# Reordering the first transfers of a two-layer hybrid decoder step on eight cores

## The chip, the cores and the metric

The kernel runs as one program on all 8 cores of one Trainium2 chip. Every core works on its own sequence, and no core talks to another. The metric is the device time of the slowest core, in microseconds (us). Repeated executions of one kernel mostly agree within a few tenths of a per cent (20 runs of the kernel before: 665.77 to 670.74 us, all within 0.5% of their median). Now and then an execution falls into a slow state, in which cores of one die show a lower clock. A median that is quoted is that of all runs.

## The reference

The reference is one inference step of a two-layer trunk (`D_MODEL = 1024`, 2048 prompt rows and 64 sample rows on each core). In each layer an input projection feeds three groups of heads, and an output projection follows:

```python
h = rms_norm(x, norm_g)
p = einsum('ntd,de->nte', h, w_in)          # IN_WIDTH = 3456 columns
a_val, a_gate, a_z, b_h, b_b, b_c, b_z, c_u, c_v, c_z = split(p)
# group A: GLU, causal depthwise conv of width 31, LayerNorm, silu, gate
a = a_val * sigmoid(a_gate)
y_a = silu(layer_norm(causal_dwconv(a_buf, a, a_conv_w) + a_conv_b)) * silu(a_z)
# group B: gated causal conv of width 3
y_b = b_b * causal_dwconv(b_buf, b_c * b_h, b_conv_w) * silu(b_z)
# group C: 128x128 causal mixing of LayerNorm(c_v) inside chunks of 128 rows
y_c = c_u * chunk_mix(layer_norm(c_v), c_ws, c_bs) * silu(c_z)
x = x + einsum('nte,ed->ntd', concat(y_a, y_b, y_c), w_out)
```

It returns the final RMS norm of both streams and the last rows of the convolution states.

## The kernel before

The rows of a core are cut into blocks of up to 512 columns. A block has three or four tiles of x, each with 128 rows; the last tile of block 1 has the 64 sample rows. The kernel records every operation with what it reads and writes. A scheduler then sets the order in each engine's queue, and adds semaphores. `after=` adds a dependence on an operation, which here serves to hold back a transfer. `mark()` is the last operation recorded for TensorE.

Each engine that starts transfers has a queue of its own to the 16 DMA engines: SyncE's (`"sp"`, q1 in the profile), ScalarE's (`"act"`, q10) and GpSimd's (`"pool"`, q0, which casts the weights to bf16 on the way).

```python
        def dma(q, out, in_, reads, writes, after=()):
            # ... S.add(q, lambda e: e.dma_start(out=out, in_=in_), ..., dma=True, after=after)

        def load_x(l, t, after=(), q="sp"):                 # one tile of x, 512 KB
            # ...
            dma(q, xr[0:r, s, :], src[r0:r0 + r, :], [] if l == 0 else [("x1", t)], [("x", s)], after)

        def load_win(l, i, after=()):                       # a piece of w_in, on GpSimd's queue
            # ...
        def load_wout(l, hf, after=()):                     # half of w_out, on GpSimd's queue
            dma("pool", w_out_sb[:, hf, :, :]..., wo_ap(w_out.tensor, l * 2 * 128 * 4096, hf, GO[l]), [],
                [("wout", hf)], after)

        def params_dma(l, after=()):                        # nine small transfers on SyncE's queue
            dma("sp", wc4[:, :], wcol[l], [], ["wc4"], after)
            dma("sp", wraw[:], c_wsT[l], [], ["wraw"], after)
            # ... wr4, gC_b, bC_b, and cbias in four parts
```

The sums of squares of a block's x are ScalarE's work. The powers `rstd` follow on GpSimd, and `h_tm = x * rstd` on VectorE:

```python
        def H_elem(l, blk):
            for j, (t, r, c0) in enumerate(blk.tiles):
                # ...
                act(h_tm[0:r, hs, :], xr[0:r, s, :], AF.Square, [("x", s)], [("htm", hs), ("ss", k)],
                    scale=1.0 / 32.0, accum=ss[0:r, k:k + 1])
                rsq(rstd[0:r, k:k + 1], ss[0:r, k:k + 1], 1, ...)   # two GpSimd instructions, save in block 0
                ts(h_tm[0:r, hs, :], xr[0:r, s, :], rstd[0:r, k:k + 1], ...)
```

The start:

```python
        for t in blocks[0].ids:
            load_x(0, t, (), "act" if t % 2 else "sp")
            if t == 1:
                dma("sp", cst[:], consts, [], ["cst"])
                dma("act", pc[:], pcols, [], ["pc"])
            if t == 2:
                xmark = [S.ops[-1].idx]
        params_dma(0)
        # ... memsets
        for i in range(len(PIECES)):                        # 13 pieces of w_in
            load_win(0, i, xmark if i >= 1 else ())
        dma("sp", a_scr.rearrange("c p t -> p c t")[:, :, 0:PADA], zpad[:], ["zpad"], [("azero",)])
        H_elem(0, blocks[0])
        # ... transposes, and the first projections of block 0 in two halves of 256 columns
```

The loop over blocks. Group A's product is stored to the scratch tensor `a_scr` and loaded back as `A4` in a layout that the depthwise convolution needs. The profile calls this load `A<-a_scr`:

```python
        for oi, (l, blk) in enumerate(order_b):
            # ...
            stage_A(l, blk, ...)                            # projections, GLU, store to a_scr
            mA = mark()
            a4 = [a4_load(l, blk, c, False) for c in range(3)]       # 12 loads on SyncE's queue
            # ... stage_Bz, stage_AZ, stage_O(*prev)
            mO = mark()
            if nxt is not None:
                for t in nxt[1].ids:
                    load_x(nxt[0], t, mA)
                    if l == 0 and blk.first and t == nxt[1].ids[2]:
                        xmark = [S.ops[-1].idx]
                if l == 0 and blk.first:
                    for hf in range(2):
                        load_wout(0, hf, xmark)             # held back until a tile of block 1's x has landed
            stage_CV(l, blk)                                # group C: variances, rstdc on GpSimd, nv
            mC = mark()
            if blk.first:
                hist_dma(l, mC)                             # loads zst, and casts it on GpSimd
            # ...
            if nxt is not None:
                H_elem(*nxt)                                # squares of the next block's x
            for c in range(3):
                stage_B(l, blk, c)
            stage_C(l, blk)
            if nxt is not None:
                pcb = [balloc() for _ in range(3)]
                convs(l, blk, a4, pcb, [0])                 # first convolution
                T(*nxt, 0); T(*nxt, 1)                      # transposes of the next block (cut: one a line)
                convs(l, blk, a4, pcb, [1])
                T(*nxt, 2); T(*nxt, 3)
                convs(l, blk, a4, pcb, [2])                 # third convolution
```

## Time and profile before

| before | value |
|---|---|
| time, median of 6 runs ahead of the prediction | 667.9 us |
| span of the profiled run, slowest core (core 6) | 665.7 us |
| spans of the eight cores | 659.7 to 665.7 us |
| TensorE busy over the span | 91% |
| TensorE busy in the first 110 us | about 70 us |

Of TensorE's 61 us of idle time, 40 us lie in the first 110 us. After that it waits for other engines for only 10.9 us, and much of the rest is the end of the kernel, where it has little left to do (11.9 us of work after 640 us). So the start is where a transfer order can matter. The table by stretches of the kernel before, core 6, shows it. Its columns are the stretch in us, its length, the busy time of each engine with its instructions, the granted share of TensorE's clock, the busy share of the DMA engines (values a little over 1 are read as full) and their rate.

```profile
core 6: us, PE busy (x) PEld busy (x) DVE busy (x) ACT busy (x) POOL busy (x), PEclk, DMA share, GB/s
0.00:20.00 20.00, 1.89 (x16) 1.62 (x16) 4.39 (x19) 7.24 (x16) 4.16 (x11) 1.00 0.71 173
20.00:40.00 20.00, 17.54 (x113) 11.42 (x114) 6.63 (x10) 5.85 (x11) 5.88 (x10) 1.00 1.04 169
40.00:60.00 20.00, 19.17 (x105) 9.78 (x102) 3.83 (x7) 1.32 (x2) 0.00 (x0) 1.00 1.03 172
60.00:80.00 20.00, 7.17 (x24) 2.75 (x24) 6.03 (x10) 8.01 (x15) 5.64 (x11) 0.66 0.84 176
80.00:100.00 20.00, 13.84 (x92) 6.12 (x92) 10.99 (x23) 2.98 (x6) 2.52 (x4) 0.83 0.73 140
```

TensorE has a hole at 60 to 80 us with only 7.17 us of work, and the clock falls there to 0.66. The list of TensorE's waits over the first 110 us of the same core names what ended each hole (what was waited for; total us; how many times; the longest):

```profile
PE pb L444 <- ACT tmp L404: 13.7, 1, 13.7
PE pb L892 <- DVE h_tm L417: 13.0, 1, 13.0
PE pb L444 <- ACT h_fm L404: 7.6, 2, 5.8
PE pb L444 <- DVE nv L420: 6.2, 1, 6.2
```

The 13.0 us are the wait for the first x, which can't be avoided entirely, since all work starts from it. The 13.7 us end with an instruction of ScalarE. The timeline of the same core (start, length, engine, line, operation, and in brackets the idle time before it and what ended it) says why ScalarE was late:

```profile
44.84 2.67 SPq L434 DMA_DIRECT2D xr<-x_in  x4
...
70.54 1.06 ACT L404 ACTIVATE h_tm<-xr 128x1024 bf16<-128x1024 f32 x1 [26.78 <-DMA xr<-x_in]
...
72.83 7.25 PE L444 MATMUL pb<-h_fm,w_in_sb 128*128 128x512 bf16 x24 [13.66 <-ACT tmp L404]
...
92.32 1.91 PE L445 MATMUL pb<-A,W 128*32 128x512 bf16 x32
94.17 7.08 PE L444 MATMUL pb<-h_fm,w_in_sb 128*128 128x512 bf16 x32
...
101.08 1.68 PE L565 MATMUL pb<-ident_bf,h_tm 128*128 128x128 bf16 x16
...
106.16 1.91 PE L445 MATMUL pb<-A,W 128*32 128x512 bf16 x32
```

ScalarE reaches the first square of block 1 at 43.8 us and stands there for 26.78 us, until that tile of x has landed. Behind it in its queue stand evacuations of PSUM that TensorE needs: instructions that copy TensorE's results out of their buffer (`pb`), so that the buffer is free again. The convolutions of block 0 are the groups of 32 matmuls `pb<-A,W`: the first starts at 92.32 us and the third at 106.16 us.

The x tile is late because it is issued only at 44.84 us, and because the DMA engines are full from 20 to 70 us (DMA share 1.02 to 1.04 in each 10 us). I counted the packets of the trace's packet records, in the microsecond from 48 to 49 us:

```
queue of GpSimd (weights):  44 packets, 36 of them of 4096 bytes
queue of SyncE:             45 packets, of 1080 bytes
```

So the DMA engines give the two queues one packet each in turn here, 4096 bytes against 1080. Three queues at work had the like: from 11 to 12 us of the same core, those of SyncE, ScalarE and GpSimd had 23, 24 and 23 packets. This does not hold everywhere in these records: at 20 to 21 us of the same core, when the weights had only begun, 389 packets of SyncE's queue (mostly of 64 and 512 bytes) passed beside 29 of the weights.

### The profile page before, as it was taken

What the parts mean: (1) busy time and instruction counts of PE and PEld (TensorE: products, weight loads), DVE (VectorE), ACT (ScalarE), POOL (GpSimd) and SP (SyncE); (2) the same over time, 40 slices, a digit from 0 to 9 for tenths busy, and PEclk for the clock granted to TensorE, in tenths of its full rate; (3) what the DMA queues carried; (4) which work ended last, traced back from release to release, by engine and by line L of the source; (5) the groups of instructions that cost most, each with busy time, mean ns of one, the idle gap of its engine ahead of it and who ended that gap; (6) DMA issues with size and microseconds to landing.
All of it is one profiled execution on the core that took longest, in us unless ns stands there. A gap on an engine that the chain in (4) does not pass through costs nothing.

```text
span 665.7 us, 11443 instructions; the slowest of 8 cores (659.7 to 665.7 us)
## 1 busy us (share of the span) xinstructions
PE 604.6 (91%) x4484; PEld 331.2 (50%) x4484; DVE 380.8 (57%) x710; ACT 268.3 (40%) x472; POOL 90.6 (14%) x163
## 2 busy tenths in 40 slices
PE   1695489999989999999998999999989999999974
PEld 0543135555545565655553544545555565665631
DVE  2240544956267475573756663977278666764774
ACT  2410516601443462272263315731474274272632
POOL 0500400201012011000223310022002002100101
PEclk9998679999999999999999999999999999999988
DMA  7899760962597359149869590532462033324202
GB/s 192 146 180 187 151 140 7 209 196 41 135 193 152 87 107 239 58 116 241 229 83 243 147 172 13 171 108 78 114 184 95 17 112 110 103 45 54 97 0 95
DMA packets 57270, 83.98 MB, mean 126 GB/s; under 512 B 8128, under 2 KB 46208, under 8 KB 56960
## 3 DMA queue, kind: packets, MB, share of 16 engines
q1 hardware_dynamic: 41168, 58.48, 31.4%
q0 software_dynamic: 11392, 19.24, 19.4%
q10 hardware_dynamic: 4656, 5.54, 3.4%
q8 instruction: 35, 0.57, 0.3%
q14 instruction: 19, 0.16, 0.1%
HBM read 80.59 MB, written 27.62 MB: 163 GB/s over the span
## 4 chain that ended last, share of the span: by engine, by line
PE 78%; DMA 10%; DVE 4%; ACT 4%; issue 2%; SPq 1%; POOL 1%; POOLq 0%; ACTq 0%; DVEq 0%
PE pb L444 68%; PE pb L445 7%; DMA xr<-x_in 6%; DMA xr<-x_scr 3%; PE pb L565 3%; ACT tmp L404 1%; ACT L404 1%; SPq L434 1%; DVE tmp L424 1%; DMA a_scr<-a_t 1%; ACT h_tm L404 1%; DVE nv L420 1%; ACT h_fm L404 0%; DVE xr L412 0%; DVE vb L773 0%
## 5 line engine op out<-in xcount | busy, mean ns | idle before, releaser
L444 PE MATMUL pb<-h_fm,w_in_sb 128*128 128x384 bf16 (+3 forms) x2032 | 372.6, 343 | 27.1 <-ACT tmp L404 17.2
L444 PEld LDWEIGHTS pb<-h_fm,w_in_sb 128*128 128x128 bf16 x2032 | 196.8, 99 | 189.8 <-ACT tmp L404 18.5
L404 ACT ACTIVATE tmp<-pb 128x384 f32<-128x384 f32 (+2 forms) x110 | 56.7, 519 | 201.5 <-PE pb L444 191.1
L444 PE MATMUL pb<-w_out_sb,mix 128*128 128x512 bf16 (+1 forms) x544 | 120.6, 382 | 4.0 <-DVE mix L412 4.0
L444 PEld LDWEIGHTS pb<-w_out_sb,mix 128*128 128x128 bf16 (+1 forms) x544 | 53.7, 99 | 68.6 <-DVE mix L412 4.4
L424 DVE SCALAR_TENSOR_TENSOR tmp<-z_ext,pc,tmp 128x384 f32<-128x384 bf16 (+1 forms) x60 | 38.1, 641 | 55.2 <-ACT tmp L404 54.6
L412 DVE TENSOR_TENSOR xr<-pb,xr 128x512 f32<-128x512 f32 (+1 forms) x68 | 46.3, 688 | 34.0 <-PE pb L444 33.6
L404 ACT ACTIVATE h_tm<-xr 128x1024 bf16<-128x1024 f32 (+1 forms) x34 | 35.7, 1051 | 64.8 <-DMA xr<-x_in 46.7
L543 POOL TENSOR_SCALAR rstd<-ss 128x1 f32<-128x1 f32 (+1 forms) x47 | 12.1, 257 | 363.3 <-ACT h_tm L404 251.8
L445 PE MATMUL pb<-A,W 128*32 128x384 bf16 (+2 forms) x1152 | 49.3, 314 | 0.0
L412 DVE TENSOR_TENSOR mix<-tmp 128x384 bf16<-128x384 f32 (+2 forms) x50 | 30.1, 602 | 27.6 <-ACT tmp L404 27.5
L424 DVE SCALAR_TENSOR_TENSOR a_t<-tmp,pb 128x384 bf16<-128x384 f32 (+1 forms) x30 | 16.8, 561 | 47.8 <-ACT tmp L404 43.2
L404 ACT ACTIVATE tmp<-xr 128x1024 bf16<-128x1024 f32 (+1 forms) x17 | 18.0, 1057 | 51.4 <-DVE xr L412 51.4
L412 DVE TENSOR_TENSOR tmp<-pb,tmp 128x384 f32<-128x384 f32 (+2 forms) x50 | 29.4, 591 | 13.4 <-PE pb L444 13.0
L417 DVE TENSOR_SCALAR h_fm<-pb,pc 128x384 bf16<-128x384 bf16 (+3 forms) x44 | 17.8, 416 | 33.2 <-PE pb L565 24.0
L445 PEld LDWEIGHTS pb<-A,W 128*32 128x32 bf16 x1152 | 24.9, 96 | 19.0 <-issue 4.5
L444 PE MATMUL pb<-w_in_sb,h_fm 128*128 128x256 bf16 (+1 forms) x272 | 31.8, 273 | 0.9 <-ACT szt L404 0.9
L404 ACT ACT_TABLE_LOAD x22 | 28.2, 1283 | 8.5 <-DMA xr<-x_in 8.2
L773 DVE RECIPROCAL vb<-vb 128x384 f32<-128x384 f32 (+2 forms) x10 | 27.9, 2792 | 4.2 <-ACT vb L404 3.9
L544 POOL TENSOR_TENSOR rstd<-rstd,mhalf 128x1 f32<-128x1 f32 (+1 forms) x47 | 29.3, 624 | 3.9
L404 ACT ACTIVATE h_fm<-pb,pc 128x384 bf16<-128x384 bf16 (+3 forms) x44 | 24.9, 580 | 12.3 <-PE pb L892 7.1
L444 PEld LDWEIGHTS pb<-w_in_sb,h_fm 128*128 128x128 bf16 (+1 forms) x272 | 26.4, 99 | 6.9 <-ACT szt L404 1.1
(73 smaller groups left out, 449.2 us busy)
## 6 DMA issues: line engine op xcount, KB each, us to landing
A<-a_scr SPq DMA_DIRECT2D x96, 103.0 KB, 4.3
w_in_sb<-w_in POOLq DMA_DIRECT2D x17, 512.0 KB, 16.4
x_scr<-xr SPq DMA_DIRECT2D x16, 512.0 KB, 4.6
xr<-x_scr SPq DMA_DIRECT2D x16, 512.0 KB, 6.3
y_o<-xr SPq DMA_DIRECT2D x16, 512.0 KB, 2.7
xr<-x_in SPq DMA_DIRECT2D x14, 512.0 KB, 14.1
w_out_sb<-w_out POOLq DMA_DIRECT2D x4, 1024.0 KB, 15.2
w_in_scr<-w_in POOLq DMA_DIRECT2D x7, 512.0 KB, 13.7
```

Source lines behind the costliest of these rows:

```text
L404: S.add("act", lambda e: e.activation(out=out, in_=in_, func=func, **kw), reads=reads, writes=writes, cost=170 + 0.833 * free_size(out) + ...
L412: S.add(eng, lambda e: e.tensor_tensor(out=out, in0=a, in1=b, op=op), reads=reads, writes=writes, cost=velem(eng, out, 1))
L417: S.add(eng, lambda e: e.tensor_scalar(out, a, s1, None, op0), reads=reads, writes=writes, cost=velem(eng, out, fast))
L420: S.add(eng, lambda e: e.tensor_scalar(out, a, s1, s2, op0, op1), reads=reads, writes=writes, cost=velem(eng, out, fast))
L424: S.add(eng, lambda e: e.scalar_tensor_tensor(out=out, in0=a, scalar=s, in1=b, op0=op0, op1=op1), reads=reads, writes=writes, cost=velem(e ...
L434: S.add(q, lambda e: e.dma_start(out=out, in_=in_), reads=reads, writes=writes, dma=True, nbytes=n * (2 if in_.dtype == BF16 else 4), afte ...
L444: return lambda e: e.matmul(out, lhsT, rhs, start=start, stop=stop)
L445: return lambda e: e.matmul(out, lhsT, rhs, start=start, stop=stop, tile_position=tp)
L543: S.add("pool", lambda e: e.tensor_scalar(out, in_, EPS, None, ALU.add), reads=rk, writes=wk, cost=300)
L544: S.add("pool", lambda e: e.tensor_tensor(out=out, in0=out, in1=mhalf[0:r, 0:nt], op=ALU.pow), reads=wk + ["mhalf"], writes=wk, cost=650)
L565: pe([(lambda e, k=k, j=j, r=r, c0=c0: e.transpose(V[:, k % 2, c0:c0 + r], h_tm[0:r, j, k * 128:(k + 1) * 128], ident_bf[0:r, 0:r])) for k ...
L773: S.add("dve", lambda e: e.reciprocal(vb[:, 0:n], vb[:, 0:n]), reads=["vb"], writes=["vb"], cost=90 + 6.4 * n)
```

## The change

The intent is to start every early transfer in the order in which it is needed. Block 0's x goes first, on SyncE's queue, with only two tables of constants (`cst`, `pc`) beside it. The first weight piece waits for x tile 0, and the others for x tile 2. The parameters and the zero pad wait until the first transposes have run, and block 1's x comes right behind them. The squares of block 1 go late in ScalarE's queue, so that ScalarE does not stand waiting for that x. In later blocks the squares of the next block get a gate (`mO`), too.

```diff
-        def load_x(l, t, after=(), q="sp"):
+        def load_x(l, t, after=()):                  # always on "sp"
 # ... act() and H_elem() get an argument after=() that is passed to the squares
         for t in blocks[0].ids:
-            load_x(0, t, (), "act" if t % 2 else "sp")
-            if t == 1:
+            load_x(0, t)
+            if t == 0:
+                x0mark = [S.ops[-1].idx]
                 dma("sp", cst[:], consts, [], ["cst"])
                 dma("act", pc[:], pcols, [], ["pc"])
             if t == 2:
                 xmark = [S.ops[-1].idx]
-        params_dma(0)
 # ...
         for i in range(len(PIECES)):
-            load_win(0, i, xmark if i >= 1 else ())
-        dma("sp", a_scr.rearrange("c p t -> p c t")[:, :, 0:PADA], zpad[:], ["zpad"], [("azero",)])
+            load_win(0, i, xmark if i >= 1 else x0mark)
 # ... in the loop over the halves hv of block 0, after the transposes:
             if hv == 0:
+                params_dma(0, mark())
+                dma("sp", a_scr.rearrange("c p t -> p c t")[:, :, 0:PADA], zpad[:], ["zpad"], [("azero",)], mark())
                 pre = [(balloc(), balloc()) for _ in range(2)]
             mT = mark()
+            if hv == 1:
+                x1mark = mT
 # ... in the loop over blocks:
                 for t in nxt[1].ids:
-                    load_x(nxt[0], t, mA)
+                    load_x(nxt[0], t, x1mark if oi == 0 else mA)
 # ...
             if nxt is not None:
-                H_elem(*nxt)
+                if oi:
+                    H_elem(*nxt, mO)
 # ...
             for c in range(3):
                 stage_B(l, blk, c)
+                if c == 1 and oi == 0:
+                    H_elem(*nxt, mark())
```

## The prediction

> **What bounds the kernel now.** The table by stretches and the timeline (slowest core, span 665.7 us) show TensorE busy almost throughout after 110 us, but only 69.6 us of the first 110. Idle there: 19 us before the first projection (20.7 us), 13.7 us at 59 to 73 us (list of waits: PE on ACT tmp), 6.2 us at 80 to 86 us (PE on DVE nv). The middle hole is a chain: ScalarE reaches block 1's first square at 44 us and sits there 26.8 us for the x tile, issued at 44.8 and landing at 70.5. Behind it PSUM is not emptied, and nv is late. The granted clock falls to 0.50 to 0.85 between 60 and 90 us.
>
> The x tile is late because the DMA engines are full: DMA share 1.0 from 20 to 70 us. The packet records show, at 48 to 49 us, 44 weight packets (4096 B, about 0.4 us each) against 45 of the other queue: one for one. [...]
>
> **What the change does.**
> 1. Start: weight piece 0 and the parameters leave the way of x. The last x tile should land near 12 instead of 17 us; weight pieces 1 to 12 should start near 10 instead of 16.8. First projection at 14.5 to 16 us, not 20.7; the second column group follows its weights (landing 17 instead of 25), so TensorE is about 8 us ahead.
> 2. Block 1's x is issued near 20 us, not 45, and lands at 45 to 60. Its squares come after block 0's second gated-conv part in ScalarE's queue. So the 26.8 us stall goes, with both holes (20 us) and part of the low clock (about 4 us).
> 3. Given back: total traffic is unchanged. The DMA engines were active about 86 of the first 95.6 us, so they cannot finish before about 89. Parameters (some 70 packets an engine) and x now stand before the A stores and loads in the same queue and take turns with weights; the output weights follow the input weights at once, 0.85 us a turn (18 packets of 8192 B a us). I count (estimate from these packet times) the last input piece at 64 to 67 us, about as before (69.5), the first convolution's A loads complete at 80 to 87, the last ones at 88 to 96.
>
> So TensorE should run out of work near 60 to 65 us and wait for A at block 0's first convolution, at a low clock again. Before, this convolution began at 92.3 us and the third at 106.2. After: first near 82 to 86, third near 95 to 100. That is 6 to 11 us of the 30 that the steps above would give. Later blocks: the squares' new gate changes little (TensorE waits only about 11 us after 110 us); plus or minus 2 us.
>
> **Time.** 658 us, 8 in 10 within 649 to 664. Faster by over 2% (below 654.5): 0.27; within 2%: 0.71; slower: 0.02.
>
> **What would show it.** First projection near 15 us; no ScalarE wait over 5 us on block 1's x; a new TensorE wait at the convolutions (L445) on DMA A<-a_scr, 10 to 20 us long; DMA share near 1.0 from 10 to 85 us; after 110 us the two traces run parallel, shifted by a constant.
>
> **What would make it wrong.** Small parameter packets may pass several at a time (64 B and 512 B ones did at 20 us): A lands earlier, the gain is 13 us or more. If served strictly one for one, bC_b and wraw could stall TensorE near 30 us. A convolution later in TensorE's queue would hide the wait.

## The result, and the profile after

| | before | after |
|---|---|---|
| median time of all runs | 667.45 us (20 runs, 665.77 to 670.74) | 674.61 us (10 runs: nine of 672.09 to 675.91, and a slow one of 736.18) |
| ratio of fast runs, 95% interval | | 1.0099 [1.0082, 1.0116] |
| spans of the eight cores, profiled run | 659.7 to 665.7 us | 661.0 to 671.4 us |
| mean of the eight spans | 663.1 us | 667.5 us |

A ratio here is always the mean time of one kernel's fast runs over that of the other's fast runs of the same rounds, so it is not quite the ratio of the medians that are quoted. Executions in which one die ran at a lower clock are left out of the means. The kernel after is about 1% slower. It stays within 2%, but the predicted gain of 10 us did not come, and even the whole range of 649 to 664 us is missed. The table by stretches after (core 0, its slowest):

```profile
core 0: us, PE busy (x) PEld busy (x) DVE busy (x) ACT busy (x) POOL busy (x), PEclk, DMA share, GB/s
0.00:20.00 20.00, 5.68 (x43) 4.35 (x44) 5.47 (x19) 8.51 (x17) 7.89 (x17) 1.00 0.86 184
20.00:40.00 20.00, 13.43 (x85) 7.93 (x82) 6.46 (x8) 4.70 (x9) 5.37 (x3) 0.83 1.05 177
40.00:60.00 20.00, 20.00 (x110) 10.35 (x110) 9.33 (x21) 5.69 (x9) 0.00 (x0) 1.00 1.05 187
60.00:80.00 20.00, 11.01 (x58) 4.88 (x56) 6.41 (x11) 5.94 (x11) 2.94 (x5) 0.91 0.81 153
80.00:100.00 20.00, 11.50 (x64) 4.53 (x64) 3.02 (x5) 1.97 (x3) 5.24 (x9) 0.66 0.63 129
```

TensorE does more work before 20 us (5.68 against 1.89 us) and between 60 and 80 us (11.01 against 7.17 us). The hole has moved behind 80 us, and the low clock of 0.66 with it. TensorE's waits over the first 110 us of that core:

```profile
PE pb L446 <- DMA A<-a_scr: 12.1, 1, 12.1
PE pb L892 <- DVE h_tm L418: 11.8, 2, 11.0
PE pb L445 <- DMA bC_b<-c_lnb: 6.6, 1, 6.6
PE pb L445 <- DVE nv L421: 5.4, 1, 5.4
PE pb L445 <- DMA w_in_sb<-w_in: 2.5, 1, 2.5
```

The wait of 13.7 us for ScalarE is gone. (`nv` are the normalised values of group C, which need the powers `rstdc`.) In its place stand 12.1 us for A, the load that the first convolution reads, and 6.6 us for a parameter (`bC_b`) that is now loaded later. The timeline of the core shows the start, the new hole and what comes after it (the same columns as before):

```profile
16.39 3.21 PE L445 MATMUL pb<-h_fm,w_in_sb 128*128 128x256 bf16 x16 [2.53 <-DMA w_in_sb<-w_in]
...
20.30 0.59 SPq L435 DMA_DIRECT2D a_scr<-zpad  x1
20.93 14.27 SPq L435 DMA_DIRECT2D xr<-x_in  x4
...
65.74 1.12 POOL L435 DMA_DIRECT2D w_out_sb<-w_out  x2 [31.95 <-DMA xr<-x_in]
...
66.40 0.32 SPq L435 DMA_DIRECT2D A<-a_scr  x1
...
88.50 3.60 PE L446 MATMUL pb<-A,W 128*32 128x512 bf16 x32 [12.10 <-DMA A<-a_scr]
92.04 8.12 PE L445 MATMUL pb<-h_fm,w_in_sb 128*128 128x512 bf16 x32
...
93.90 0.27 POOL L429 CAST zs_ext<-zst 128x96 bf16<-128x96 f32 x1 [25.07 <-DMA zst<-st_bT]
...
101.24 1.69 PE L566 MATMUL pb<-ident_bf,h_tm 128*128 128x128 bf16 x16 [1.08 <-DVE tmp L413]
...
106.33 1.91 PE L446 MATMUL pb<-A,W 128*32 128x512 bf16 x32
```

The first projection starts at 16.39 us, not 20.66. Block 1's x is issued at 20.93 us, not 44.84, and ScalarE waits for it only 0.3 us. Yet the first convolution starts at 88.50 us, the third at 106.33 us. The third is no earlier than the 106.16 us of before.

A core is a sample of one of eight, and the cores differ by several us at the start. I therefore took the same milestones from the trace of every core, and averaged them. This table is used in all that follows (us). "x3" is the landing of the last tile of block 0's x, "x4" that of the first tile of block 1's x, "A" the landing of the last load for the first convolution, "T" the start of block 1's transposes. (A recorded expectation below reads the third convolution 0.2 us later than this table.)

| kernel | x3 | x4 | A | first conv | T | third conv | span |
|---|---|---|---|---|---|---|---|
| before | 16.6 | 66.9 | 64.2 | 88.8 | 97.5 | 102.6 | 663.1 |
| after | 13.1 | 57.3 | 86.8 | 86.9 | 99.1 | 104.8 | 667.5 |
| params_act | 18.8 | 34.5 | 83.0 | 83.1 | 96.5 | 102.9 | 666.3 |
| zpad_act | 13.6 | 49.4 | 84.6 | 84.7 | 96.4 | 101.7 | 665.6 |
| no_late_gate | 13.8 | 57.8 | 87.3 | 87.4 | 99.3 | 105.2 | 667.0 |
| gate_only | 17.4 | 67.2 | 64.8 | 89.3 | 98.0 | 103.1 | 665.3 |
| zst_early | 13.4 | 57.6 | 87.4 | 87.5 | 99.3 | 104.9 | 665.8 |
| squares_late | 17.1 | 66.6 | 64.1 | 82.7 | 99.6 | 106.8 | 667.0 |
| before_wout | 17.0 | 67.2 | 64.6 | 89.1 | 97.9 | 103.0 | 663.3 |
| after_wout | 13.2 | 57.5 | 74.0 | 74.2 | 86.4 | 92.5 | 655.6 |
| act_wout_late_xlate | 18.4 | 65.9 | 60.9 | 64.5 | 88.0 | 95.5 | 657.4 |
| act_wout_late | 18.5 | 34.3 | 72.6 | 72.7 | 83.9 | 89.2 | 650.3 |
| best1z | 18.7 | 34.4 | 72.7 | 72.8 | 83.5 | 88.5 | 650.2 |
| best3 | 19.0 | 34.6 | 72.7 | 75.9 | 70.7 | 81.1 | 642.7 |

In the kernels before, gate_only, squares_late and before_wout the first convolution starts long after its A. In the others, save act_wout_late_xlate and best3, it starts within 0.2 us of A. There it is A that it waits for.

The mean span grows by 4.4 us. Of this, 2.2 us are there by the third convolution (102.6 to 104.8). Another 1.8 us come at one later place: between two fixed transposes around the turn from layer 0 to layer 1, the mean time goes from 71.1 to 72.9 us. The timed 6.6 us (1% of 667 us) are more than the mean's 4.4, because the time is that of the slowest core. The slowest stands 3.9 us above the mean after, and 2.6 us before. Why the spread grows I did not look into.

### The profile page after: what moved, and what is told of

The parts are those of the page before. It is cut to its first block, busy times and chain, and to the rows that moved or that the text cites. A ratio compares the mean times of both kernels' runs of the same rounds, so it can differ in the third digit from the quotient of the medians.

```text
span 671.4 us, 11464 instructions; the slowest of 8 cores (661.0 to 671.4 us)
## 1 busy us (share of the span) xinstructions
PE 610.2 (91%) x4484; PEld 332.4 (50%) x4484; DVE 382.1 (57%) x710; ACT 271.3 (40%) x472; POOL 103.4 (15%) x163
## 4 chain that ended last, share of the span: by engine, by line
PE 76%; DMA 12%; DVE 3%; ACT 3%; SPq 2%; POOL 2%; issue 1%; POOLq 0%; ACTq 0%; DVEq 0%
PE pb L445 67%; DMA a_scr<-a_t 7%; PE pb L446 7%; PE pb L566 3%; SPq L435 2%; DMA zst<-st_bT 2%; DMA w_in_sb<-w_in 1%; POOL rstd L545 1%; ACT L404 1%; DMA xr<-x_in 1%; ACT tmp L404 1%; DVE tmp L425 1%; POOL rstd L544 1%; DVE nv L421 1%; DVE tmp L413 0%
## 5 line engine op out<-in xcount | busy, mean ns | idle before, releaser
L446 PE MATMUL pb<-A,W 128*32 128x384 bf16 (+2 forms) x1152 | 51.0, 321 | 12.1 <-DMA A<-a_scr 12.1
L544 POOL TENSOR_SCALAR rstd<-ss 128x1 f32<-128x1 f32 (+1 forms) x47 | 13.5, 288 | 292.5 <-ACT tmp L404 221.9
L418 DVE TENSOR_SCALAR h_tm<-xr,rstd 128x1024 bf16<-128x1024 f32 (+1 forms) x34 | 25.6, 754 | 28.0 <-POOL rstd L545 25.6
L446 PEld LDWEIGHTS pb<-A,W 128*32 128x32 bf16 x1152 | 25.4, 97 | 32.0 <-issue 18.5
L413 DVE TENSOR_TENSOR mix<-tmp 128x384 bf16<-128x384 f32 (+2 forms) x50 | 29.9, 599 | 19.0 <-ACT tmp L404 18.4
L404 ACT ACTIVATE tmp<-xr 128x1024 bf16<-128x1024 f32 (+1 forms) x17 | 17.9, 1054 | 47.3 <-DVE xr L413 47.3
L545 POOL TENSOR_TENSOR rstd<-rstd,mhalf 128x1 f32<-128x1 f32 (+1 forms) x47 | 33.1, 705 | 3.7
L404 ACT ACTIVATE cbh<-pb,pc 128x384 bf16<-128x384 f32 (+2 forms) x30 | 18.4, 613 | 32.6 <-PE pb L446 32.1
L404 ACT ACTIVATE tmp<-z_ext,pc 128x384 f32<-128x384 bf16 (+1 forms) x30 | 18.7, 632 | 30.9 <-DVE z_ext L413 24.2
## 6 DMA issues: line engine op xcount, KB each, us to landing
A<-a_scr SPq DMA_DIRECT2D x96, 103.0 KB, 4.0
```

What stands on the lines that cost most here:

```text
L404: S.add("act", lambda e: e.activation(out=out, in_=in_, func=func, **kw), reads=reads, writes=writes, cost=170 + 0.833 * free_size(out) + ...
L413: S.add(eng, lambda e: e.tensor_tensor(out=out, in0=a, in1=b, op=op), reads=reads, writes=writes, cost=velem(eng, out, 1))
L418: S.add(eng, lambda e: e.tensor_scalar(out, a, s1, None, op0), reads=reads, writes=writes, cost=velem(eng, out, fast))
L446: return lambda e: e.matmul(out, lhsT, rhs, start=start, stop=stop, tile_position=tp)
L544: S.add("pool", lambda e: e.tensor_scalar(out, in_, EPS, None, ALU.add), reads=rk, writes=wk, cost=300)
L545: S.add("pool", lambda e: e.tensor_tensor(out=out, in0=out, in1=mhalf[0:r, 0:nt], op=ALU.pow), reads=wk + ["mhalf"], writes=wk, cost=650)
```

## The experiments

My theory after the result was that the A loads are late because they stand behind other transfers in SyncE's queue, and take turns with large weight packets of GpSimd's queue. A rival was the new gate on the squares. A second rival was that the start's order itself is at fault. In each diff below, "after" or "before" says which kernel was edited. All runs gave correct results.

### params_act: parameters and zero pad on ScalarE's queue

```diff
 # from after
-    NDMA = {"sp": 24, "pool": 24, "act": 8}          # semaphores for transfers in flight
+    NDMA = {"sp": 24, "pool": 24, "act": 24}
+        params_dma(0, (), "act")                     # right behind the loads of block 0's x
+        dma("act", a_scr...[:, :, 0:PADA], zpad[:], ["zpad"], [("azero",)])
-                params_dma(0, mark())                # at hv == 0
-                dma("sp", a_scr...[:, :, 0:PADA], zpad[:], ["zpad"], [("azero",)], mark())
```

> The kernel after the change, but block 0's parameters and the zero pad are issued at once on ScalarE's DMA queue, so that nothing small stands before block 1's x in SyncE's queue. Theory 'turns' (each small packet in front of x costs one full weight packet, about 0.42 us, about 80 of them an engine): block 1's first x tile lands near 36 to 42 us instead of 58.7, the wait of TensorE on bC_b (6.6 us) is gone, the wait on A<-a_scr shrinks, and the kernel is 8 to 20 us faster than the one after the change (655 to 667 us). Rival 'late gate' (the loss is made by the squares' gate in later blocks): within 3 us of the kernel after the change, about 672 to 676 us. Rival 'bandwidth only' (total bytes bound the start, order does not matter): x earlier, but the first convolution still begins at 86 to 90 us and the time stays at 670 or more.

Measured: 673.05 us against 667.85 us of before, ratio 1.0072 [1.0047, 1.0097]. This cannot be told from after's 1.0099, and the theory's 655 to 667 us were missed. The first tile of block 1's x lands at 34.5 us instead of 57.3, so the parameters and the pad were what held it. (They are also issued earlier in this run, so the figure is not of the queue alone.) But x of block 0 lands 5.7 us later, the first projection starts 3.6 us later (19.3 instead of 15.7 us in the mean), and A lands only 3.8 us earlier, at 83.0 us. TensorE's wait for A is even longer, as core 3 shows in the list of its waits:

```profile
PE pb L446 <- DMA A<-a_scr: 17.8, 1, 17.8
```

It follows that early x does not help by itself. Something else holds A.

### no_late_gate and gate_only: the gate on the squares of later blocks

```diff
 # no_late_gate, from after
-                    H_elem(*nxt, mO)
+                    H_elem(*nxt)
 # gate_only, from before (with the argument after= in act and H_elem)
-                H_elem(*nxt)
+                H_elem(*nxt, mO if oi else ())
```

> The kernel after the change without the gate on the squares of blocks after the first (the gate of block 1's squares stays). Theory 'late gate': the TensorE wait on nv in the first block of layer 1 (2.1 us, with a low clock after it) is gone, from the transposes of the 5th to those of the 6th block takes 71.0 us as before instead of 72.9, and the kernel comes back to 667 or below, 6 to 8 us faster than after the change. Theory 'turns' for the bulk: only 2 to 4 us faster, 670 to 672 us, with the first 100 us unchanged.

> The kernel before with one part of the change alone: the squares of blocks 2 and later gated on the output projection's last matmul. If the gate costs by itself: 2 to 5 us slower than before (669.5 to 672.5 us), with an nv wait in the first block of layer 1. If it costs only together with the rest: within 1 us of before.

Measured: no_late_gate 671.62 against 667.85 us, ratio 1.0057 [1.0036, 1.0078]. gate_only 671.93 against 667.85 us, ratio 1.0062 [1.0040, 1.0084]. So the gate alone costs about 0.6% on the kernel before, and taking it out of the kernel after gives back about 0.4% of the 1.0%. In gate_only nothing moves at the start: the third convolution is at 103.1 us (102.6 before). The mean time between the two transposes at the turn of the layers is 73.1 us (71.1 before); without the gate it is 71.3 us. The cause can be read on GpSimd. First the kernel before, core 6, timeline of GpSimd at that place:

```profile
385.73 0.23 POOL L543 TENSOR_SCALAR rstdc<-mv 128x4 f32<-128x4 f32 x1 [0.18 <-DVE mv L724]
386.05 1.05 POOL L544 TENSOR_TENSOR rstdc<-rstdc,mhalf 128x4 f32<-128x4 f32 x1
393.50 0.27 POOL L428 CAST zs_ext<-zst 128x96 bf16<-128x96 f32 x1 [6.40 <-DMA zst<-st_bT]
```

Then the same place in gate_only, core 0:

```profile
386.65 0.81 POOL L544 TENSOR_SCALAR rstdc<-mv 128x4 f32<-128x4 f32 x1
391.93 0.27 POOL L429 CAST zs_ext<-zst 128x96 bf16<-128x96 f32 x1 [4.46 <-DMA zst<-st_bT]
392.17 1.05 POOL L545 TENSOR_TENSOR rstdc<-rstdc,mhalf 128x4 f32<-128x4 f32 x1
```

`rstdc` takes two instructions. With the gate, the scheduler puts the cast of `zst` between them. The cast waits for a transfer, and the second half of `rstdc` waits with it. TensorE then waits for `nv` in gate_only (its list of waits from 380 to 402 us):

```profile
PE pb L445 <- DVE nv L421: 2.4, 1, 2.4
```

The kernel after has the same wait with 2.1 us, the kernel before has none there, and the granted clock in after and gate_only is 0.91 from 390 to 410 us.

### zpad_act: only the zero pad on ScalarE's queue

```diff
 # from after
+        dma("act", a_scr...[:, :, 0:PADA], zpad[:], ["zpad"], [("azero",)])   # at the start
-                dma("sp", a_scr...[:, :, 0:PADA], zpad[:], ["zpad"], [("azero",)], mark())
```

> The kernel after the change with only the zero pad (24 packets of 64 B an engine, 24 KB in all) moved to the start on ScalarE's queue. Theory 'turns': block 1's first x tile lands 7 to 10 us earlier (near 49 to 51 instead of 58.7 us) although only 24 KB of 2 MB were taken out of its way, and the kernel is 2 to 5 us faster than after the change. If bytes counted, 24 KB would move it by 0.1 us and the time by nothing.

Measured: 670.93 against 667.85 us, ratio 1.0037 [1.0014, 1.0060] (one slow run of 768.15 us is in the median, not in the ratio). The pad is 24 KB, which is 24 packets of 64 bytes on each DMA engine. Moving it brings the first tile of block 1's x from 57.3 to 49.4 us, A from 86.8 to 84.6 us and the third convolution from 104.8 to 101.7 us. In the kernel after I counted the packets between 45 and 46 us: 46 of the weight queue (42 of 4096 bytes) against 46 of 64 bytes. There a packet of 64 bytes cost its queue the same turn as one of 4096. This is one part of the loss, but A is still at 84.6 us.

### zst_early: the load that the cast waits for, earlier

```diff
 # from after
-        def hist_dma(l, after=()):
+        def hist_dma(l, after=(), zafter=()):
-            dma("sp", zst[:], st_bT[l], [], ["zst"], after)
+            dma("sp", zst[:], st_bT[l], [], ["zst"], zafter)
-                hist_dma(l, mC)
+                hist_dma(l, mC, mC if l == 0 else mA)
```

> The kernel after the change with one small load of layer 1 (the carried states of group B) issued earlier, so that GpSimd's cast of it no longer holds the variance of group C behind it. If the cost of the late squares' gate is this wait: 71.0 to 71.6 us from the 5th to the 6th block's transposes instead of 72.9, no nv wait there, 2 to 4 us faster than after the change (670 to 672.5). If it is something else (low clock, DMA): no change, 673 to 676.

Measured: 672.17 against 669.84 us, ratio 1.0033 [1.0006, 1.0061]. The time between the two transposes at the turn of the layers is 70.9 us (after 72.9, before 71.1), although the gate is still there. The wait for `nv` is gone from the list of 380 to 402 us. The start is as in after (third convolution at 104.9 us). So the gate itself costs nothing measurable there: its cost is the place of the cast in GpSimd's queue, and the late `zst`.

### squares_late: block 1's squares late, all else as before

```diff
 # from before
             if nxt is not None:
-                H_elem(*nxt)
+                if oi:
+                    H_elem(*nxt)
 # ...
                 stage_B(l, blk, c)
+                if c == 1 and oi == 0:
+                    H_elem(*nxt, mark())
```

> The kernel before with one part of the change alone: block 1's squares stand later in ScalarE's queue (after the second gated-conv part of block 0), nothing else moved. If ScalarE's stall on block 1's x was what the start lost: the 13.7 us TensorE wait on ACT tmp goes, block 1's transposes (97.5 us before, mean over cores) begin 5 to 15 us earlier and the kernel is 5 to 12 us faster than before (656 to 663). Rival: the DMA engines bound the start whatever the order, TensorE then waits for A loads or transposed x instead, and the time stays within 2 us of before.

Measured: 674.20 against 669.84 us, ratio 1.0064 [1.0038, 1.0090]. Neither expectation was met: ScalarE's longest wait for x falls from 26.8 to 5.7 us (core 1), the first convolution starts 6 us earlier (82.7 instead of 88.8 us), and yet the transposes are 2.1 us later and the third convolution 4.2 us later than before. GpSimd's list of waits over the first 115 us (core 1) tells why, and TensorE's, which follows, shows the effect:

```profile
POOL w_out_sb L435 <- DMA xr<-x_in: 46.2, 1, 46.2
POOL zs_ext L429 <- DMA zst<-st_bT: 19.9, 1, 19.9
```

```profile
PE pb L445 <- DVE nv L421: 13.6, 1, 13.6
...
PE pb L566 <- DVE tmp L413: 9.7, 1, 9.7
```

GpSimd issues the output weights, and that issue waits 46.2 us for a tile of block 1's x. Everything recorded behind it stands, `rstdc` among it. The stall has moved from ScalarE's queue to GpSimd's. The kernel after has the same with 32.0 us (the line at 65.74 us in its timeline): what `rstdc` needs was ready at 59.8 us, `rstdc` started at 67.46 us, behind that issue, and 5.4 us of the delay reach TensorE as its wait for `nv`. Moving the squares and the output weights together in the kernel before was not tried.

### after_wout and before_wout: only the output weights later

The output weights are 2 MB in packets of 8192 bytes. Both kernels hold them back until the third tile of block 1's x has landed. As x is early now, they come early too, right when A is loaded. In the kernel after I counted 17 packets of them against 17 packets of A (1080 bytes) in the microsecond from 74 to 75 us, and 234 packets of A's queue from 87 to 88 us, when the weight queue was empty. These two runs move them alone:

```diff
 # from after, and the same from before
-                if oi == 0:                          # before: if l == 0 and blk.first
-                    for hf in range(2):
-                        load_wout(0, hf, xmark)
 # ...
                 convs(l, blk, a4, pcb, [0])
+                if oi == 0:
+                    for hf in range(2):
+                        load_wout(0, hf, mark())
```

> The kernel after the change with one thing moved: the output weights (2 MB in bf16) are gated on block 0's first convolution instead of on block 1's x. Parameters stay in front of x. Theory 'output weights in turn with A' : A of the first convolution complete near 70 to 76 us instead of 86.8 (mean over cores), block 1's transposes near 84 to 90 instead of 99.1, 8 to 14 us faster than after the change (660 to 667 us; the late gate still costs 3 to 4). Rival 'parameters in front of x' as the main cost: A complete no earlier than 82, gain under 4 us.

> The kernel before with the output weights gated on block 0's first convolution, nothing else. If the output weights' moment were the whole of the gain found so far, this kernel alone would be 8 us or more faster than before. Theory: in the kernel before the start is bound by ScalarE's stall on x and the nv wait, not by A, so it changes by less than 3 us (666 to 671).

Measured: after_wout 661.97 against 667.33 us, ratio 0.9901 [0.9843, 0.9959] (one slow run of 741.75 us is in the median, not in the ratio). before_wout 668.15 against 667.33 us, ratio 0.9997 [0.9947, 1.0048]. In after_wout, A lands at 74.0 us instead of 86.8. The first convolution, the transposes and the third convolution all come 12 to 13 us earlier, as does the end (655.6 instead of 667.5 us, mean span). The loads of A are issued no earlier than in after (from 68.4 us, against 65.6), but take 5.6 us from the first issue to the landing, not 21.2. What is left of TensorE's wait for A on core 4 is this:

```profile
PE pb L446 <- DMA A<-a_scr: 5.1, 1, 5.1
```

On the kernel before the same move does nothing. Its last A load comes 12.6 us earlier (79.8 instead of 92.4 us), but A of the first convolution had landed at 64 us in any case, more than 24 us ahead of its use. This is the run that decides. It shows that the loss of the kernel after is an interaction: the change makes x early, x releases the output weights, and these take turns with A, which the change has put behind the parameters and x.

Without the output weights beside it, A still lands 9.8 us later than before (74.0 against 64.2 us). That part lies ahead of the loads, and the traces show it: A is stored to `a_scr` first, and is loaded only when the store has landed. The store is issued at about the same time in both kernels (32.3 us before, 33.5 after). It lands at 42.2 us before and at 65.5 us after, where it stands behind block 1's x in SyncE's queue (the last tile lands at 65.2 us).

The move takes away two things at once, the output weights' packets and the wait that GpSimd had in its queue. A's landing is due to the first, as the times of issue above show. TensorE's 5.4 us for `nv` came before the wait for A, so I take them to be hidden by it; no run of its own tells the two apart.

### act_wout_late and act_wout_late_xlate: is early x worth anything now?

```diff
 # act_wout_late, from after: the edits of params_act and of after_wout, and no gate in later blocks
-                    H_elem(*nxt, mO)
+                    H_elem(*nxt)
 # act_wout_late_xlate: the same, and in addition
-                    load_x(nxt[0], t, x1mark if oi == 0 else mA)
+                    load_x(nxt[0], t, mA)
```

> The kernel after the change with parameters and zero pad on ScalarE's queue, no gate on later blocks' squares, and the output weights gated on block 0's first convolution instead of block 1's x. Theory 'turns' (the A loads wait because every 1080-B packet pays a full turn of 0.4 us beside input weights and 0.85 us beside output weights): first convolution's A complete near 70 to 75 us instead of 83, block 1's transposes begin near 78 to 86 instead of 96 to 99, and the kernel is 10 to 20 us faster than before (648 to 658). Rival 'bandwidth only' (same bytes, so the same end of the start): transposes at 94 or later, 663 us or more.

> As act_wout_late, but block 1's x is gated on the end of block 0's stage A, as before the change, so it stands behind the first A loads in the queue and not in front. If early x costs because it stands in front of the A loads: first convolution's A complete near 52 to 60 us, x lands at 64 to 72, transposes at 74 to 82, and the kernel is 3 to 8 us faster than act_wout_late (643 to 652). If early x helps: 3 us or more slower than act_wout_late.

Measured: act_wout_late 654.57 against 669.84 us, ratio 0.9764 [0.9739, 0.9789]. act_wout_late_xlate 660.76 us, ratio 0.9859 [0.9830, 0.9887]. With x late, A lands at 60.9 us and the first convolution starts at 64.5 us, 8 us earlier than with x early. But the transposes come at 88.0 us, 4.1 us later. TensorE's list of waits in act_wout_late_xlate (core 4) shows the new hole, which I had not expected to be so large:

```profile
PE pb L566 <- DVE tmp L413: 15.0, 1, 15.0
```

So early x is worth about 1% once A is not starved. The intent of the change was sound, and its price was elsewhere.

### best1z and best3: filling what is left

```diff
 # best1z, from act_wout_late: layer 0's zst at the start, on ScalarE's queue; its cast gated on mC
+        dma("act", zst[:], st_bT[0], [], ["zst"])
 # best3, from best1z: the first convolution of block 0 behind stage_C's last projection (conv and pe get after=)
-                convs(l, blk, a4, pcb, [0])
+                convs(l, blk, a4, pcb, [0], mark() if oi == 0 else ())
```

> As act_wout_late, with the small load of group B's carried states at the start on ScalarE's queue, so that GpSimd's cast does not wait for it behind the A loads and hold block 1's variances. If that holds block 1's transposes (83.9 us mean): they begin 2 to 4 us earlier, 651 to 654 us. Else no change (654 to 656).

> As best1z, with block 0's first convolution placed after group C's projections in TensorE's order. If TensorE's wait on A (6.5 us at 68 us) is then filled with those 7 us of projections: block 1's transposes near 75 to 80 us, the third convolution near 84 to 86 instead of 89.4, 3 to 6 us faster than best1z (645 to 651). If the input weights (last at 68 us) bind instead: the same within 1 us.

Measured: best1z 654.14 against 667.33 us, ratio 0.9788 [0.9738, 0.9839]; best3 646.39 us, ratio 0.9683 [0.9619, 0.9747]. best1z is no better than act_wout_late (transposes at 83.5 instead of 83.9 us): with A in its place, the late cast of `zst` no longer ends the last wait there. best3 changes the order on TensorE alone. The scheduler had put the first convolution ahead of other work that was ready, so TensorE waited for A with work behind it. With the convolution behind the projections, the wait for A is gone. The list of waits over the first 110 us (core 6) has three lines:

```profile
PE pb L896 <- DVE h_tm L418: 13.1, 1, 13.1
PE pb L445 <- DMA w_in_sb<-w_in: 5.8, 2, 4.9
PE pb L567 <- DVE tmp L413: 1.0, 1, 1.0
```

Its table by stretches, same core, in the two stretches where before and after have their holes:

```profile
60.00:80.00 20.00, 19.00 (x153) 8.85 (x154) 12.15 (x21) 9.01 (x17) 4.66 (x8) 1.00 0.78 153
80.00:100.00 20.00, 20.00 (x144) 10.16 (x137) 12.36 (x22) 13.78 (x21) 1.94 (x3) 1.00 0.87 130
```

TensorE is busy for 39 of these 40 us at full clock. best3 beats both kernels, by 3.2% the one before.

## Why the prediction was wrong

**What held.** The start: the first projection was predicted at 14.5 to 16 us and came at 15.7 us in the mean (16.4 on core 0), with the last x tile at 13.1 us (predicted 12). The stall of ScalarE went, from 26.8 to 0.3 us. Block 1's x was predicted at 45 to 60 us; its first tile came at 57.3 us in the mean, its last at 65.2 us, which is past the range. The last weight piece was predicted at 64 to 67 us; it came at 63.6 us, just below. A was predicted at 80 to 87 us for the first convolution and came at 86.8; the last A load was predicted at 88 to 96 us and came at 91.4. The new wait for A was predicted as 10 to 20 us and was 12.1 us. The stall on `bC_b` was named as what could go wrong, and it took 6.6 us. So the mechanism, early x against late A, was seen.

**What failed** is the step "After: first near 82 to 86, third near 95 to 100", and with it "That is 6 to 11 us of the 30". The third convolution came 2.2 us later than before in the mean (104.8 against 102.6), where the middle of the prediction had it 8.7 us earlier (97.5 against 106.2). These 10.9 us have three parts:

1. *The baseline, 3.6 us.* "Before, this convolution began at 92.3 us and the third at 106.2" was read from core 6, the slowest. The mean of the eight cores is 88.8 and 102.6 us. A gain against the unlucky core is partly a gain against its luck.
2. *The first convolution, 2.9 us.* It came at 86.9 us, where the middle of the range was 84. A landed at the late end of its own predicted range, and the convolution follows it within 0.1 us. I had counted the turns of the output weights (0.85 us each, an estimate from 18 packets a microsecond in the kernel before) but did not ask why they should be in flight just then. The change releases them by making x early. after_wout shows what that costs: 12.8 us of A's landing.
3. *The distance from the first to the third convolution, 4.4 us.* I took 13 to 14 us, about as before (13.8). It was 17.9 us. On core 0 the distance is 17.83 us, on core 6 of before 13.84 us. Of the 4.0 us between them, 2.7 us are the low clock after the hole: 32 matmuls of the convolution took 3.60 instead of 1.91 us, and the next 32 projections 8.12 instead of 7.08 us. Another 1.1 us are the wait ahead of block 1's transposes, which comes after GpSimd's 25.1 us at the cast of `zst`. I had written "at a low clock again", but put no time to it. In the trace the wait of 12.1 us is followed by matmuls at 1.88 times their length, and the granted clock is 0.50 from 85 to 90 us (0.66 over 80 to 100 us).

**The second failed step** is "the squares' new gate changes little; plus or minus 2 us". gate_only shows 0.62%, which is 4.1 us of 667.85. In the mean of the cores it is 2.1 us of span, at the edge of what was said, of which 2.0 us lie between the two transposes at the turn of the layers. It also falsifies "after 110 us the two traces run parallel": by the end the kernel after has lost another 2.2 us in the mean, 1.8 of them at this place. ("DMA share near 1.0 from 10 to 85 us" did not hold either: it was 0.81 from 60 to 80 us.) I had looked at whether TensorE waits for the squares, and not at what the gate does to the order of GpSimd's queue. zst_early shows that it is this order.

**Where the expected gain went.** The change takes away a stall of ScalarE and puts a later A in its place, at the same point of TensorE's queue. Three costs are each shown by a run: the output weights released early (after_wout, 12.8 us of A's landing; the ratio goes from 1.0099 to 0.9901), the pad's small packets in front of x (zpad_act, 2.2 us of A's landing and 3.1 us at the third convolution), and the gate (no_late_gate, 1.0057; zst_early, 1.0033). No run takes away just these three; act_wout_late, which moves the parameters too, is at 0.9764. Taking away the pad or the gate alone left the kernel slower than before (1.0037 and 1.0057); moving the output weights was the step that made it faster. In params_act, x came 23 us earlier still, and the time cannot be told from that of the kernel after.

**Still open.** The slowest core stands further above the mean after the change (3.9 against 2.6 us), for which I have no cause. best3 was not tried with block 0's x alone in front. It gives up the early start of the kernel after (x3 at 19.0 instead of 13.1 us), so a few us more may be there; no run shows it.

## What to carry to other kernels

When a transfer is moved earlier, look up everything that is gated on its landing: it moves earlier too, and may land on top of what is needed next. Count transfers that share DMA engines in packets, not bytes, where the trace shows them taking turns: here a 64-byte packet in front took a turn against a 4096-byte one (46 against 46 in a microsecond). ScalarE waiting for data (26.8 us) and GpSimd waiting only to issue a transfer (32.0 us) both held back what stood behind them, so a stall that is removed from one queue has to be looked for in the next; and a baseline should be the mean of all cores, not the slowest one.
